# A hybrid decoder trunk: the mixer's parts in another order

## The chip, the cores and the metric

The kernel runs on one core of a Trainium2 chip. The metric is the device time of one execution in microseconds. In the profile PE is TensorE, PEld its weight loads, DVE VectorE, ACT ScalarE, POOL GpSimd, and SP the engine whose queue issues most DMAs; L152 is line 152 of the kernel's file.

## The reference

The trunk has two layers on a sequence of 512 tokens of width 1024. Cut to what matters here, one layer is:

```python
x = x + 0.5 * swiglu(rms_norm(x, ffn1_norm), ffn1_w_in, ffn1_w_out)
z = rms_norm(x, mix_norm) @ mix_w_in          # 1024 -> 772 (FoX) + 768 (MoBA) + 1824 (RWKV)
y = concat([fox_mixer(z_fox), rwkv7_mixer(z_rwkv), moba_mixer(z_moba)]) @ mix_w_out
x = x + y
x = x + memory_cross_attention(rms_norm(x), rms_norm(mem), ...)
x = x + 0.5 * swiglu(rms_norm(x, ffn2_norm), ffn2_w_in, ffn2_w_out)
```

- `fox_mixer`: causal attention of 4 heads of 64 with normalised q and k, and a bias of cumulated log-sigmoid gates (4 columns of z).
- `rwkv7_mixer`: 8 heads of 64. Each projected column is mixed with its value one token earlier. From r, k, v, a decay (a tanh of 64 columns, through w2), a rate a (64 columns, through a2) and a gate g (160 columns, through g2) a state of 64 x 64 per head is carried over the tokens: `state = state * w + (state @ -kk) (kk*a)^T + v k^T`, and `y = state @ r`; then a group norm, a bonus term and the gate.
- `moba_mixer`: attention of 4 heads with rotary positions; at 512 tokens the selected blocks and the own block together are plain causal attention.
- `memory_cross_attention`: 4 heads of 128 over 256 memory tokens.

## The kernel before

Activations lie transposed, features on partitions, 512 tokens along the free axis. A product of full precision is made of three matmuls (`three`, L152 to L154) of a high and a low half of weights and activations. `weights` loads a weight block of 512 KB by SP's queue into `wraw` (three buffers), ACT copies the high half `whi` (L145) and DVE subtracts it for the low half `wlo` (L146), two buffers each.

**Projections of the mixer.** A narrow projection (`zproj`) makes 128 columns for all 512 tokens: 8 pieces of the contraction, 24 matmuls of 512 columns into one PSUM bank. RWKV has 15 of them: R, K and V for each of four pairs of heads (R0 to V3, `rwkv_z`), and three in `rwkv_prep`: the first for decay and rate (`tw`), the second for most of the gate (`gs0`), the third for the rest of the gate and FoX's four gate columns, whose cumulated sums `fox_gates` makes. FoX's q and k are four more (fq0, fq1, fk0, fk1, `heads_t`). A wide projection (`ztok`, L948 to L950) makes 256 columns with the tokens on partitions, 96 matmuls of 256 columns: fv, mv (`values`), mq and mk (`heads`).

**RWKV by pairs.** Each pair of heads passes through six stages, written as generators: `s` (`rwkv_scaled`: norm of k at L641, decay and rate at L650, scaled operands), `g` (`rwkv_gram`, L717: products of the operands, written to DRAM (`scA`), read back as blocks of 16 (`A`), inverted on POOL in 30 small operations (L282) and sent back through DRAM to `Tf` and `Pf`), `r` (`rwkv_rows`), `i` (`rwkv_inverse`, from L809), `t` (`rwkv_transitions`) and `y` (`rwkv_states`: eight steps of the state in a row at L900 and L902, the group norm with DVE's scaling at L920, transposes at L924, and the gate at L930 and L931). `fNM` is one unit of FoX attention: query block N, pair of heads M, with scores (L1034), softmax, transposes (L1022) and the product with the values (L1046).

**The order.** `ORDER` lists the parts of the mixer. `order` gives the n-th part a priority of 1000 n less a lead from `PRI` by its kind; a planner that estimates the time of each instruction then lays the instructions of each engine in order, by priority among those that it takes to be ready. On the chip each engine goes through its list in that order. `ORDER2` does the same for the stage behind (`31` and the like are MoBA units, `m` one step of the memory's keys and values `mem_kv`, `c` a split of outputs, `w` an output projection, `x` the return of x), and `ORDER3` for the cross-attention.

**Memory.** The mixer's eight PSUM banks are `acc` (1), `sp` (2), `tx` (1), `ty` (2) and `ts` (2). Projections use `acc`, but K0 goes to `sp` and the second of `rwkv_prep` to `tx` (`ACC`). `tx` serves stage s, `ty` stages g, r and i, `ts` stages t and y; attention in this stage puts scores, transposes and outputs into `sp`. The next stage has `acc`, `po`, `sp` and `pt`, two banks each. `RPW` and `BPW` say in which of three pools a bank lies, and pools of the same number follow each other in the same memory: a bank of the next stage waits for the one that lay there. `LATE` does the same for SBUF tiles: those of pool 0 lie where the next stage's memory keys and values come, those of pool 2 farther behind. `p` and `pT`, the tiles of every attention unit and of q and k heads, have one buffer each in this stage.

Of the kernel before, what the change touches and what calls it, by code (L numbers as in the profile page):

```python
# [25 lines left out]
PRI = {"s": 1500, "g": 6000, "r": 6000, "i": 10000, "t": -3000, "y": 6000, "p": 4000, "R": 1500, "q": -1500, "f": -1500, "V": 6000, "g1": 2500}  # L26
# [7 lines left out]

ORDER = ("R0 V0 K0 p R1 K1 s0 fk1 g0 V1 r0 fq1 i0 K2 t0 fk0 R2 V2 fq0 s1 g1 r1 i1 fv y0 t1 K3 s2 R3 g2 "
         "f01 r2 mk y1 f11 f00 i2 mq V3 t2 s3 g3 r3 f20 f10 i3 y2 t3 f30 f21 y3 f31 mv")


ORDER2 = "31 11 10 m c0 01 21 00 c1 c2 m c4 x c5 c3 m c6 w3 m 20 m w6 m 30 w4 c7 w1 w5 w2 w0"

ORDER3 = "sum spread z1 z0 n1 z2 n0 m n2 02 z3 00 n3 12 03 10 13 01 11"
BP = {"acc": 2, "po": 2, "sp": 2, "pt": 2}

TAGS = {"s": "tx", "g": "ty", "r": "ty", "i": "ty", "t": "ts", "y": "ts"}

LATE = {"y2": 1, "G": 0, "Pf": 1, "KX": 1, "tk1": 0, "V2": 0, "gs0": 2, "gs1": 2, "ER": 1, "BN": 1, "KV": 2, "AR": 2, "tk2": 1, "g2": 1, "var": 2, "DC": 2, "p": 2, "a": 2, "zr": 0, "e": 0, "lw": 1, "zv": 1, "zk": 0}
RPW = {"ts": 0, "sp": 1, "acc": 0, "tx": 1, "ty": 1}
BPW = {"acc": 0, "sp": 2, "pt": 0, "po": 1}  # L50

RW = {"e": 2, "tk1": 2, "tk2": 2, "zr": 2, "zv": 2, "ER": 2, "zk": 2, "BN": 2}
RP = {"acc": 1, "tx": 1, "ty": 2, "ts": 2, "sp": 2}
# [2 lines left out]
ACC = {"K0": "sp", "p1": "tx"}  # L56
# [59 lines left out]
class Trunk:  # L116
# [405 lines left out]
        nc.vector.scalar_tensor_tensor(out, z[:m, 1:], self.dpar[:m, l, 14 + i:15 + i], out, op0=ALU.mult, op1=ALU.add)  # L522

    def rwkv_prep(self, l, ap, rp, at, ab):
        nc, rw = self.nc, self.rw
        w = self.ins['mix_w_in'][l]
        self.tw = rw.tile([P, S], F32, name="tw", tag="tw")
        self.acc = ACC.get("p0", "acc")
        ps = self.zproj(ap, *self.weights(w[:, Z_LO:Z_LO + P]), P)
        self.shift(l, 12, ps, P, self.tw)  # L530
        nc.scalar.activation(self.tw[0:64], self.tw[0:64], AF.Tanh)
        self.gs = []
        for i, m in ((0, P), (1, 32)):
            g = rw.tile([P, S], F32, name=f"gs{i}", tag=f"gs{i}")
            self.acc = ACC.get(f"p{i + 1}", "acc")
            if i == 0:
                ps = self.zproj(ap, *self.weights(w[:, Z_LO + P:Z_LO + 256]), P)
            else:
                ps = self.zproj(ap, *self.weights(w[:, Z_LO + 256:Z_LO + 288], w[:, 768:772]), 36)
                self.fox_gates(l, ps, rp, at, ab)  # L540
            self.shift(l, 13 + i, ps, m, g[:m])
            nc.scalar.activation(g[:m], g[:m], AF.Tanh, scale=0.5)
            nc.vector.tensor_scalar(g[:m], g[:m], 0.5, 0.5, op0=ALU.mult, op1=ALU.add)
            self.gs.append(g)

    def fox_gates(self, l, ps, rp, at, ab):

# [594 lines left out]
    def mixer_and_xattn(self, l):  # L1142
        tc, nc = self.tc, self.nc

        def sb(name, bufs=1):
            return tc.tile_pool(name=name, bufs=bufs, reuse_waits="tile")

        def pp(name, bufs=1):
            return tc.tile_pool(name=name, bufs=bufs, space=PSUM, reuse_waits="tile")
# [4 lines left out]
        fv = xt[:, 4:6, :].rearrange("p a (b c) -> p (a b) c", c=256)  # L1154
        cqk = xt[:, 6:8, :].rearrange("p a b -> p (a b)").bitcast(BF16).rearrange("p (i a s) -> p i a s", i=2, a=2)
        self.cq, self.ck = cqk[:, 0], cqk[:, 1]
        with sb("raw") as raw:
            mq = raw.tile([P, 2, S], F32, name="mq", tag="mq")
            mk = raw.tile([P, 2, S], F32, name="mk", tag="mk")
            mv = raw.tile([P, NT, 256], F32, name="mvv", tag="mvv")  # L1160
# [6 lines left out]
            with sb("rw") as rw0, sb("rwm") as rw1, sb("rwl") as rw2, pp("rp") as rp0, pp("rps") as rp1, pp("rpt") as rp2:  # L1167
                rp = self.tp = TagPool((rp0, rp1, rp2), RP, where=RPW)
                self.rw = at = TagPool((rw0, rw1, rw2), RW, where=LATE)
                w = self.ins['mix_w_in'][l]  # L1170
                sts = [{} for _ in range(4)]


                steps, begun = [self.norm_sum, self.norm_spread], []

                def z(nm, hp):
                    g = self.rwkv_z(l, hp, rp, "RKV".index(nm))
                    next(g)
                    if steps:
                        steps.pop(0)(self.bank(TAGS["s"], 1)[:, 0])  # L1180
                        begun.append((g, nm, hp))
                        if steps:
                            return
                    for g, nm, hp in begun or [(g, nm, hp)]:
                        sts[hp][nm] = next(g)
                    begun.clear()

                def go(*parts):

                    gens = [f(l, hp, sts[hp]) for f, hp in parts]  # L1190
                    while gens:
                        gens = [g for g in gens if next(g, gens) is not gens]

                early = [0, 0]

                def attend(o):

                    fox, t, pr = o[0] == "f", int(o[1]), int(o[2])
                    q, k, v = (fq, fk, fv) if fox else (mq, mk, mv)
                    if not fox:  # L1200
                        early[pr] += 1
                        assert early[pr] == t + 1
                    self.causal(at, rp, q, k, v, t, pr,
                                lambda ps: self.cp("fo", q[:, pr, t * P:(t + 1) * P], ps), fox)

                def unit_t(*a):
                    self.heads_t(*a)()

                def unit(*a):
                    self.heads(*a)()  # L1210
                scaled, gram, rows = self.rwkv_scaled, self.rwkv_gram, self.rwkv_rows
                inverse, trans, states = self.rwkv_inverse, self.rwkv_transitions, self.rwkv_states
                parts = {"fv": lambda: self.values(l, 0, rp, fv),
                         "mq": lambda: unit(w, 772, 0, rp, at, rp, mq, 64, self.rope(l, 0)),
                         "mk": lambda: unit(w, 772, 1, rp, at, rp, mk, 64, self.rope(l, 1)),
                         "mv": lambda: self.values(l, 772, rp, mv),
                         "p": lambda: self.rwkv_prep(l, rp, rp, at, rp)}
                stages = {"s": scaled, "g": gram, "r": rows, "i": inverse, "t": trans, "y": states}
                for a in range(2):
                    parts[f"fq{a}"] = lambda a=a: unit_t(w[:, a * P:(a + 1) * P], rp, at, rp, fq[:, a], 64, self.dpar[:, l, 12:13])  # L1220
                    parts[f"fk{a}"] = lambda a=a: unit_t(w[:, 256 + a * P:384 + a * P], rp, at, rp, fk[:, a], 64,
                                                         self.par('fox_k_gain', l))
                for o in self.order(ORDER, PRI, lambda o: "q" if o in parts and o != "p" else o[0]):
                    self.acc = ACC.get(o, "acc")
                    if o in parts:
                        parts[o]()
                    elif o[0] in "KRV":
                        z(o[0], int(o[1]))
                    elif o[0] in "fb":
                        attend(o)  # L1230
                    else:
                        go(*[(stages[a[0]], int(a[1])) for a in o.split("+")])
            self.acc = "acc"
            with sb("kv") as kv, pp("bp") as bp0, pp("bps") as bp1, pp("bpt") as bp2:
                bp = TagPool((bp0, bp1, bp2), BP, {"st": "po"}, BPW)
                mem = self.mem_kv(l, kv, bp)
                bank = lambda m: bp.tile([P, 512], F32, name="sp", tag="sp")

                with sb("at") as at_, sb("yy") as yy:
# [4 lines left out]
                    at = TagPool(at_, {**AT, "mx": 2, "sm": 2, "hr": 2})  # L1244
# [5 lines left out]
                    done = set()  # L1250
                    for o in self.order(ORDER2, PRI2, lambda o: "a" if o[0] in "0123" else o[0]):
                        if o == "m":
# [5 lines left out]
                        elif o[0] == "w":  # L1258
                            m = int(o[1])
# [97 lines left out]
```

## Time and profile before

| | us |
|---|---|
| median of 3 runs | 2590.47 |
| lowest and highest | 2580.43, 2592.95 |
| the profiled execution: its time | 2590.88 |
| the profiled execution: span from first to last instruction | 2589.1 |
| PE busy | 2497.2 (96% of the span) |
| DVE, ACT, POOL busy | 1346.6, 846.9, 493.0 |

The span is what the trace covers, and the time of the execution is a little longer. Matmuls are pipelined, so a busy PE is not a PE at its peak; the granted clock tells how fast it was allowed to run.

### The profile page before, as it was taken

What the parts mean: (1) busy time and instruction counts of PE and PEld (TensorE: products, weight loads), DVE (VectorE), ACT (ScalarE), POOL (GpSimd) and SP (SyncE); (2) the same over time, 40 slices, a digit from 0 to 9 for tenths busy, and PEclk for the clock granted to TensorE, in tenths of its full rate; (3) what the DMA queues carried; (4) which work ended last, traced back from release to release, by engine and by line L of the source; (5) the groups of instructions that cost most, each with busy time, mean ns of one, the idle gap of its engine ahead of it and who ended that gap; (6) DMA issues with size and microseconds to landing.
All of it is one profiled execution on the core that took longest, in us unless ns stands there. A gap on an engine that the chain in (4) does not pass through costs nothing.

```text
span 2589.1 us, 35163 instructions
## 1 busy us (share of the span) xinstructions
PE 2497.2 (96%) x13976; PEld 2025.7 (78%) x13976; DVE 1346.6 (52%) x2503; ACT 846.9 (33%) x1337; POOL 493.0 (19%) x610
## 2 busy tenths in 40 slices
PE   8999998899999899999999999999999899999999
PEld 7888876787667788888888888767877677888887
DVE  6444445666755654344444444465666666543444
ACT  4222233233343342222332222333333433422222
POOL 4212120232210122020221211202322110221211
PEclk9999999998889999999999999999978999999999
DMA  4333342221213133333333333422212121333332
GB/s 143 104 98 94 96 130 69 66 59 43 64 34 92 53 96 90 104 93 98 95 94 100 94 98 94 121 75 58 67 34 56 56 78 45 110 98 98 95 95 88
DMA packets 434880, 218.41 MB, mean 84 GB/s; under 512 B 63856, under 2 KB 428828, under 8 KB 434716
## 3 DMA queue, kind: packets, MB, share of 16 engines
q1 hardware_dynamic: 431948, 212.36, 28.9%
q10 hardware_dynamic: 2448, 2.76, 0.3%
q8 instruction: 110, 1.80, 0.3%
q0 software_dynamic: 320, 1.05, 0.1%
q14 instruction: 54, 0.44, 0.1%
HBM read 205.64 MB, written 10.49 MB: 83 GB/s over the span
## 4 chain that ended last, share of the span: by engine, by line
PE 86%; DVE 6%; POOL 3%; DMA 2%; ACT 2%; issue 1%; SPq 1%; POOLq 0%; ACTq 0%; DVEq 0%
PE acc L152 22%; PE acc L154 22%; PE acc L153 22%; PE po L1046 2%; PE sp L1034 1%; POOL P L282 1%; PE pt L1022 1%; PE acc L950 1%; PE acc L948 1%; PE acc L949 1%; POOL T L282 1%; DVE wlo L146 1%; ACT whi L145 1%; PE ts L857 1%; PE ty L717 1%
## 5 line engine op out<-in xcount | busy, mean ns | idle before, releaser
L145 ACT ACTIVATE whi<-wraw 128x1024 fp32r<-128x1024 f32 (+3 forms) x386 | 390.3, 1013 | 1142.0 <-PE acc L153 1043.3
L152 PE MATMUL acc<-xh,whi 128*128 128x512 f32 (+1 forms) x1776 | 699.9, 394 | 21.9 <-DVE p L496 7.3
L154 PE MATMUL acc<-xh,wlo 128*128 128x512 f32 (+1 forms) x1776 | 695.8, 392 | 1.3 <-DVE wlo L146 1.3
L153 PE MATMUL acc<-xl,whi 128*128 128x512 f32 (+1 forms) x1776 | 694.8, 391 | 0.0
L146 DVE TENSOR_TENSOR wlo<-wraw,whi 128x1024 fp32r<-128x1024 f32 (+3 forms) x386 | 540.3, 1401 | 100.3 <-ACT whi L145 91.4
L152 PEld LDWEIGHTS acc<-xh,whi 128*128 128x128 f32 (+1 forms) x1776 | 334.4, 188 | 97.6 <-ACT whi L145 9.1
L154 PEld LDWEIGHTS acc<-xh,wlo 128*128 128x128 f32 (+1 forms) x1776 | 334.2, 188 | 75.5 <-DVE wlo L146 2.6
L153 PEld LDWEIGHTS acc<-xl,whi 128*128 128x128 f32 (+1 forms) x1776 | 334.6, 188 | 69.7
L342 POOL TENSOR_TENSOR up<-up,g 128x512 f32<-128x512 f32 x88 | 118.4, 1346 | 999.2 <-ACT whi L145 901.1
L152 PE MATMUL acc<-th,whi 128*128 128x512 f32 x704 | 274.4, 391 | 1.0 <-ACT whi L145 1.0
L154 PE MATMUL acc<-th,wlo 128*128 128x512 f32 x704 | 275.0, 392 | 0.2
L153 PE MATMUL acc<-tl,whi 128*128 128x512 f32 x704 | 274.0, 389 | 0.0
L295 DVE SCALAR_TENSOR_TENSOR x<-acc,x 128x512 f32<-128x512 f32 x96 | 66.0, 691 | 277.2 <-PE acc L154 277.2
L341 DVE TENSOR_TENSOR up<-acc,rsb 128x512 f32<-128x512 f32 x88 | 60.8, 691 | 278.5 <-PE acc L154 278.5
L338 DVE TENSOR_TENSOR g<-acc,rsb 128x512 f32<-128x512 f32 x88 | 60.8, 691 | 191.0 <-PE acc L154 188.0
L154 PEld LDWEIGHTS acc<-th,wlo 128*128 128x128 f32 x704 | 132.1, 188 | 31.5 <-DVE wlo L146 4.2
L152 PEld LDWEIGHTS acc<-th,whi 128*128 128x128 f32 x704 | 132.2, 188 | 30.5 <-ACT whi L145 4.0
L153 PEld LDWEIGHTS acc<-tl,whi 128*128 128x128 f32 x704 | 132.2, 188 | 27.4
L240 POOL TENSOR_TENSOR sqacc<-sqacc,sq 128x512 f32<-128x512 f32 x48 | 75.4, 1571 | 381.6 <-ACT sq L239 245.9
L346 POOL TENSOR_TENSOR tl<-up,th 128x512 fp32r<-128x512 f32 x88 | 128.5, 1461 | 65.5 <-ACT th L345 65.5
L345 ACT ACTIVATE th<-up 128x512 fp32r<-128x512 f32 x88 | 55.8, 634 | 120.8 <-POOL up L342 120.8
L948 PE MATMUL acc<-whi,xh 128*128 128x256 f32 x256 | 76.9, 300 | 0.7 <-DVE zt L520 0.7
(351 smaller groups left out, 3109.1 us busy)
## 6 DMA issues: line engine op xcount, KB each, us to landing
wraw<-in_ffn_w_in_dram SPq DMA_DIRECT2D x176, 512.0 KB
wraw<-in_ffn_w_out_dram SPq DMA_DIRECT2D x64, 512.0 KB
wraw<-in_mix_w_in_dram SPq DMA_DIRECT2D x52, 512.0 KB
wraw<-in_ffn_w_out_dram SPq DMA_DIRECT2D x32, 384.0 KB
wraw<-in_xattn_w_kv_dram SPq DMA_DIRECT2D x16, 512.0 KB
wraw<-in_mix_w_out_dram SPq DMA_DIRECT2D x16, 384.0 KB
scx<-x SPq DMA_DIRECT2D x16, 256.0 KB
x<-scx SPq DMA_DIRECT2D x16, 256.0 KB
```

The lines of the kernel that those rows point to most:

```text
L145: nc.scalar.activation(hv, v, AF.Copy)
L146: nc.vector.tensor_sub(lv, v, f32(hv))
L152: mm(ps, lh, rh, start=start, stop=False)
L153: mm(ps, lh, rl, start=False, stop=False)
L154: mm(ps, ll, rh, start=False, stop=stop)
L240: (nc.vector if m == KC - 1 else nc.gpsimd).tensor_tensor(self.sqacc, self.sqacc, sq, op=ALU.add)
L295: self.nc.vector.scalar_tensor_tensor(xm, ps, coef, xm, op0=ALU.mult, op1=ALU.add)
L338: nc.vector.tensor_tensor(g, pss[0], rsb, op=ALU.mult)
L341: nc.vector.tensor_tensor(up, pss[1], rsb, op=ALU.mult)
L342: nc.gpsimd.tensor_tensor(up, up, g, op=ALU.mult)
L346: nc.gpsimd.tensor_tensor(tl, up, f32(th), op=ALU.subtract)
L948: mm(o, a, wh[:, kk, :], start=k == 0, stop=False)
```

## The change

`ORDER` and `ORDER2` are other lists. `rwkv_prep` becomes a generator of three steps, so that its projections are three parts of the list (p0, p1, p2) in place of one (p); each keeps its bank. K0 and R0 stand first, p0 and V0 next, and then stage s of pair 0. FoX's, MoBA's and the gate's projections stand farther behind. Four of the small placements change with it.

```diff
-ORDER = ("R0 V0 K0 p R1 K1 s0 fk1 g0 V1 r0 fq1 i0 K2 t0 fk0 R2 V2 fq0 s1 g1 r1 i1 fv y0 t1 K3 s2 R3 g2 "
-         "f01 r2 mk y1 f11 f00 i2 mq V3 t2 s3 g3 r3 f20 f10 i3 y2 t3 f30 f21 y3 f31 mv")
+ORDER = ("K0 R0 p0 V0 s0 K1 R1 g0 p1 r0 V1 i0 p2 t0 s1 K2 g1 R2 y0 r1 V2 i1 fk1 s2 t1 fq1 K3 g2 R3 y1 r2 V3 i2 fv "
+         "s3 t2 f01 fk0 g3 fq0 y2 r3 f11 f00 mk i3 f10 f21 mq mv t3 f20 f31 y3 f30")
-ORDER2 = "31 11 10 m c0 01 21 00 c1 c2 m c4 x c5 c3 m c6 w3 m 20 m w6 m 30 w4 c7 w1 w5 w2 w0"
+ORDER2 = "m 31 11 m 10 c0 01 m 21 c1 c2 00 c4 x m c5 c3 w3 20 c6 m w6 30 m w4 c7 w1 w5 w2 w0"
-LATE = {... "p": 2, "a": 2, ...}
-RPW = {"ts": 0, "sp": 1, "acc": 0, "tx": 1, "ty": 1}
-BPW = {"acc": 0, "sp": 2, "pt": 0, "po": 1}
+LATE = {... "p": 2, "pT": 2, "a": 2, ...}
+RPW = {"acc": 0, "tx": 0, "ty": 0, "sp": 1, "ts": 2}
+BPW = {"acc": 0, "pt": 0, "sp": 1, "po": 2}
...
     def rwkv_prep(self, l, ap, rp, at, ab):
-        self.acc = ACC.get("p0", "acc")
         ps = self.zproj(ap, *self.weights(w[:, Z_LO:Z_LO + P]), P)
         self.shift(l, 12, ps, P, self.tw)
         nc.scalar.activation(self.tw[0:64], self.tw[0:64], AF.Tanh)
+        yield
         self.gs = []
         for i, m in ((0, P), (1, 32)):
-            self.acc = ACC.get(f"p{i + 1}", "acc")
...
             self.gs.append(g)
+            yield
...
+                prep = self.rwkv_prep(l, rp, rp, at, rp)
-                         "p": lambda: self.rwkv_prep(l, rp, rp, at, rp)}
+                         **{f"p{i}": lambda: next(prep) for i in range(3)}}
-                for o in self.order(ORDER, PRI, lambda o: "q" if o in parts and o != "p" else o[0]):
+                for o in self.order(ORDER, PRI, lambda o: "q" if o in parts and o[0] != "p" else o[0]):
```

## Rows read from the trace of the kernel before

**Rows 1.** The page: span, and granted clock in 40 slices (tenths).
```profile
span 2589.1 us, 35163 instructions
...
PEclk9999999998889999999999999999978999999999
```

**Rows 2.** Stretches: length, busy (count) of PE PEld DVE ACT POOL, PEclk, DMA.
```profile
387.00:600.00 213.00, 197.33 (x1456) 158.79 (x1456) 129.34 (x320) 67.30 (x106) 42.56 (x95) 0.96 0.26 64
600.00:686.00 86.00, 83.07 (x830) 69.00 (x828) 62.24 (x162) 28.57 (x64) 19.55 (x45) 0.94 0.15 34
686.00:757.50 71.50, 60.71 (x500) 38.47 (x499) 39.36 (x117) 28.69 (x66) 15.64 (x33) 0.78 0.15 43
757.50:870.00 112.50, 108.01 (x594) 84.85 (x593) 68.37 (x165) 46.02 (x92) 13.09 (x9) 0.99 0.30 92
...
1666.80:1880.00 213.20, 196.53 (x1453) 158.14 (x1454) 129.25 (x320) 67.32 (x106) 42.66 (x95) 0.96 0.26 64
1880.00:1966.00 86.00, 81.60 (x779) 68.32 (x779) 57.73 (x150) 26.81 (x60) 18.32 (x46) 0.86 0.15 35
1966.00:2039.00 73.00, 63.82 (x555) 45.05 (x555) 41.25 (x128) 30.40 (x69) 15.19 (x30) 0.84 0.17 41
```

**Rows 3.** The stretch from 600, instructions of L152, then of L948: PE, PEld.
```profile
600.00:757.50 157.50, 3.33 (x8) 1.50 (x8) 0.87 0.15 38
...
600.00:757.50 157.50, 16.09 (x54) 10.45 (x54) 0.87 0.15 38
```

**Rows 4.** Timeline of POOL: start, us, engine line op out<-in shapes xcount [idle before <-releaser].
```profile
475.84 0.22 POOL L282 TENSOR_TENSOR T<-A,P 64x15 f32<-64x15 f32 x1 [6.65 <-DMA A<-scA]
...
480.68 1.35 POOL L282 TENSOR_TENSOR P<-P,T 64x63 f32<-64x63 f32 x1
...
617.98 0.41 POOL L282 TENSOR_TENSOR P<-P,T 64x63 f32<-64x63 f32 x1
```

**Rows 5.** Timeline of PE, pair 0: last gram matmuls and first of the inverse.
```profile
465.17 1.79 PE L717 MATMUL ty<-ER,B 64*128 64x128 f32 x16 [1.00 <-DVE BN L721]
...
496.64 0.33 PE L809 MATMUL ty<-Tf,tk 64*64 64x64 f32 x2 [2.52 <-DMA Tf<-scT]
```

**Rows 6.** Timeline of PE, end of layer 0's mixer.
```profile
727.33 1.12 PE L1034 MATMUL sp<-fox 64*128 64x512 f32 x2
...
731.87 0.60 PE L1022 MATMUL pt<-ident,p 128*128 128x128 f32 x4
...
736.33 1.09 PE L1046 MATMUL po<-pT,fox 128*64 128x128 f32 x8
...
751.07 1.09 PE L924 MATMUL ts<-ident,tk 128*128 128x128 f32 x4 [4.14 <-DVE tk L920]
...
755.79 1.97 PE L1022 MATMUL pt<-ident,p 128*128 128x128 f32 x8
757.55 1.91 PE L1075 MATMUL acc<-ident,mtk 128*128 128x128 f32 x8
```

**Rows 7.** Timeline of DVE: a weight split, and a MoBA unit's last scaling.
```profile
480.62 1.23 DVE L146 TENSOR_TENSOR wlo<-wraw,whi 128x1024 fp32r<-128x1024 f32 x1 [0.22 <-ACT whi L145]
...
745.59 0.35 DVE L1019 TENSOR_SCALAR p<-p,sm 128x256 f32<-128x256 f32 x1
```

**Rows 8.** Timeline of PE: V0's first matmul, and the first of pair 0.
```profile
396.54 0.50 PE L152 MATMUL acc<-xh,whi 128*128 128x512 f32 x1 [2.35 <-DVE zt L520]
...
441.74 0.95 PE L641 MATMUL tx<-blk,e 128*128 128x2 f32 x8
```

**Rows 9.** Timeline of PE: a projection's first matmul, and what follows its last.
```profile
447.82 0.50 PE L152 MATMUL acc<-xh,whi 128*128 128x512 f32 x1 [0.43 <-DVE p L496]
...
453.43 0.95 PE L502 MATMUL sp<-blk,p 128*128 128x2 f32 x8
```

**Rows 10.** Two stretches around a fall of the clock, columns as in rows 2.
```profile
580.00:589.20 9.20, 9.20 (x104) 8.19 (x103) 6.57 (x11) 4.43 (x7) 2.92 (x2) 1.00 0.17 47
589.20:599.40 10.20, 10.20 (x51) 8.18 (x50) 4.75 (x12) 1.32 (x2) 1.30 (x2) 0.50 0.21 63
```

More of the change, by code (lines that the diff above doesn't have):

```diff
@@ L46 @@
 TAGS = {"s": "tx", "g": "ty", "r": "ty", "i": "ty", "t": "ts", "y": "ts"}
-LATE = {"y2": 1, "G": 0, "Pf": 1, "KX": 1, "tk1": 0, "V2": 0, "gs0": 2, "gs1": 2, "ER": 1, "BN": 1, "KV": 2, "AR": 2, "tk2": 1, "g2": 1, "var": 2, "DC": 2, "p": 2, "a": 2, "zr": 0, "e": 0, "lw": 1, "zv": 1, "zk": 0}
-RPW = {"ts": 0, "sp": 1, "acc": 0, "tx": 1, "ty": 1}
-BPW = {"acc": 0, "sp": 2, "pt": 0, "po": 1}
+LATE = {"y2": 1, "G": 0, "Pf": 1, "KX": 1, "tk1": 0, "V2": 0, "gs0": 2, "gs1": 2, "ER": 1, "BN": 1, "KV": 2, "AR": 2, "tk2": 1, "g2": 1, "var": 2, "DC": 2, "p": 2, "pT": 2, "a": 2, "zr": 0, "e": 0, "lw": 1, "zv": 1, "zk": 0}
+RPW = {"acc": 0, "tx": 0, "ty": 0, "sp": 1, "ts": 2}
+BPW = {"acc": 0, "pt": 0, "sp": 1, "po": 2}
 RW = {"e": 2, "tk1": 2, "tk2": 2, "zr": 2, "zv": 2, "ER": 2, "zk": 2, "BN": 2}
```

## The prediction

> **What bounds the kernel now.** I read the page first: the span is 2589.1 us, and TensorE's granted clock dips only in two places [rows 1]. They are the two layers' mixers, so I cut one into stretches and looked at two losses in each: the time in which PE is not busy, and the share of the clock not granted [rows 2]. The two levels are 1.2 and 2.4 GHz, so a granted 0.78 is full clock for 56% of a stretch and half clock for 44%; where PE is busy, one minus the granted clock, times the length, is the time that half clock costs. In layer 0:
>
> - 387 to 600: idle 213.0 - 197.3 = 15.7, clock 0.04 x 213 = 8.5, together 24.2 us or 11.4%.
> - 600 to 686: 2.9 + 5.2 = 8.1 us, 9.4%.
> - 686 to 757.5: 10.8 + 15.7 = 26.5 us, 37%.
>
> Layer 1 gives 25.2 (11.8%), 16.4 (19%) and 20.9 us (29%). A mixer thus loses 58.8 and 62.5 us, 121 together. The end is set by PE's work plus such losses, and the worst stretch is the last of each mixer.
>
> Why the last: a mixer has 19 narrow projections (24 matmuls, 8 of them on line 152) and 4 wide ones (96 matmuls, 32 on line 948). Behind 600 us lie 8 of 152 and 54 of 128 [rows 3], one narrow and 1.7 wide. What is left for the end is the chain of RWKV's pair 3, with attention. One pair's chain is long and mostly not PE's: in pair 0 the last gram matmuls begin at 465.17, the blocks are back from DRAM at 475.84, POOL inverts, and the inverse begins at 496.64 [rows 4, 5]: 30 us. At the very end PE waits 4.14 us for DVE's scaling behind the group norm [rows 6]. The next stage can't fill that wait: a MoBA unit's probabilities are ready at 745.94, yet the transposes of the MoBA units start at 755.79, right behind the last `ts` work, and the memory's at 757.55 [rows 6, 7]. Their banks lie where `ts` and `acc` were, and pair 3 holds `ts` to the end.
>
> **The change part by part.**
>
> *Instructions.* The yields and the new lists add and remove none: the same 23 projections, weight loads on SP's queue and gates, and the same banks for K0 and p1. All is order, memory placement, and what these let overlap.
>
> *Pair 0 begins earlier.* Before, its first own matmul comes at 441.74 [rows 8], behind R0, V0, K0, p0, p1, p2, R1 and K1. Now `s0` needs K0, R0, p0 and V0 only. A narrow projection takes 5.6 us (447.82 to 453.43) [rows 9], four fewer some 22 us, so I expect it at about 420. The chains of pairs 0 and 1 can then be covered by K1, R1, V1, p1, p2, K2, R2 and V2, 45 us against a chain's 30. On SP's queue a pair's block transfers now stand among more weight loads, and a load waits for the split of older weights; behind it the blocks wait, then POOL, then PE. The bound above is the 2.52 us wait for `Tf` [rows 5] once more in each of three pairs, 7.6 us a layer and 15 in all; below, nothing. I take nothing, since pair 0 already has loads around it and its wait is in the loss of the first part, which I use below.
>
> *The start.* Before, R0 and V0 share one `acc` bank, and V0 waits 2.35 us for R0's eviction, which waits for the broadcast norm [rows 8]. Now K0 (bank `sp`) goes first, R0 follows at once, and the norm can be there at its end; p0 still waits for R0's eviction, as the 0.43 us at 447.82 [rows 9]. Gain 1.9 us a layer, 3.8 in all; bounds 0 and 4.7.
>
> *Projections moved back.* fk0, fq0, mk, mq and mv now stand behind pair 3's gram. A wide matmul has half the columns of a narrow one, so I estimate 96 x 5.6/24/2 = 11.2 us for a wide projection. Three wide and two narrow are 45 us of dense matmuls in the last part, where before 5.6 + 1.7 x 11.2 = 25 us stood. Pair 3's own R, K and V come earlier, so its chain can run beside them.
>
> *The hand-over.* `acc`, `tx` and `ty` now lie under the next stage's `acc` and `pt`, and `ts` under its `po`; `pT` moves to the late memory. So the memory's projections, now first in the next list, need not wait for pair 3's last matmul nor the last `pT`. They are work moved, not saved: the stretch that they leave loses only 4.5 + 1.1 of 112.5 us [rows 2] and keeps the output projections. If it runs short of cover there, the loss reappears there; the bound is the 4.14 us wait of before.
>
> *POOL.* An inversion is 30 small operations in a row. One of them took 1.35 us in pair 0 while DVE split weights (480.62 to 481.85) and 0.41 in pair 2, away from projections [rows 4, 7]. Three splits beside an inversion are some 3 us more. I take nothing, hidden by PE's work as long as that lasts; uncovered in one pair of each layer it is +6. The Trainium skill (SBUF — State Buffer, section "SBUF: two separate sides") gives the cause: a VectorE operation with two SBUF inputs and a GpSimd operation that reads SBUF shut each other out for a whole instruction. By that rule each projection's weight split holds up the inversion beside it, which speaks against this change, and the trace agrees at 480.68; the sum by it would be the 6 us higher.
>
> *The sum.* PE's work at full clock is 370.5 - 58.8 = 311.7 us in layer 0 and 372.2 - 62.5 = 309.7 in layer 1. Dense matmuls beside pairs' chains is what the first part has today, and it loses 11.4 to 11.8%. I take 11.6% for the whole new mixer: 311.7/0.884 = 352.6 (-17.9) and 309.7/0.884 = 350.3 (-21.9). With the start, -43.6 us. The profiled execution took 2590.88 us (its span and 1.8), against a median of 2590.47; 2590.9 - 43.6 = 2547, and I say 2548. Bounds of the share: the 5% of the stretch behind the mixer gives -89, today's 16% nothing.
>
> **The rivals.**
>
> *The half clock only moves (2584).* Idle time is not all that matters to the clock: from 580.0 to 589.2 PE was busy 9.20 of 9.20 us, with 104 mostly small matmuls, and ran the next 10.2 us at half clock [rows 10]. With two pairs' small matmuls side by side and fewer projections among them, half clock may go to the first part. Then only idle time is saved: 27.3 us in the later parts, which at the first part's 7.4 to 7.8% would be 24, so -3, and the start: 2584. Against it: R, K, V and p still lie in the first part.
>
> *The clock follows idle time alone (2525).* Then filling PE's long waits gives all half clock back: (8.5 + 5.2 + 15.7) + (8.5 + 12.0 + 11.7) = 61.6 us, and the start: 2525. Against it stands the fall at 589.2, with no wait before it. The Trainium skill (TensorE: Matmul & The Clock Gate, section "Why this matters for your kernels") advises against idle gaps between bursts of matmuls; the row at 589.2 shows a fall without one, so this gets little.
>
> *Attention piles up at the end (2615, slower).* In this stage `p` and `pT` have one buffer each, and attention, fk, fq, mk and mq all pass through them. A FoX unit of four blocks runs from 727.33 to 737.42, 10.1 us, in which PE has 2 x 1.12 + 2 x 0.60 + 2 x 1.09 = 5.6 us of its own [rows 6]. FoX needs fk1, fq1, fv and p2, which now come later. If its units fall behind, the last ones stand alone: each then costs 4.5 us idle and, at half clock, 5.6 more. The last stretches lose 26.5 + 20.9 = 47.4 us now. It decides from 47.4/2/10.1 = 2.3 units alone behind a layer's last dense projection: three make 61, +13 or 2604; four make 81, +33 or 2624. For it: the list ends t3, f20, f31, y3, f30. Against: memory projections and MoBA units can now run beside them.
>
> **How the numbers follow.** The forecast's case (2530 to 2570) 0.55; half clock moves (2570 to 2600) 0.18; clock follows idle time (below 2530) 0.13; pile-up (above 2600) 0.14. A measurement tells this kernel from no change at about 0.5%, 13 us: below 2577.5 or above 2603.4. Faster are the first and third and a little of the second, 0.69; within 0.5% most of the second and the edge of the last, 0.18; slower 0.13. The range takes in the bounds of SP, POOL and the start around the forecast and the next cases, cutting the outer part of the two far ones: 2520 to 2600.
>
> **What would show it.** Right: pair 0's first square-sum matmul near 420; no 2.35 us wait behind the norm; memory transposes before the last `ts` matmul; some 352 us from the first projection to the end of pair 3; clock losses of a layer well below 29 us. Wrong: clock losses as large but earlier; a wait for `Tf` in every pair; FoX units alone at the end.

## The result: slower, and the profile after

The changed kernel takes 2664.93 us (median of 4, 2657.91 to 2670.61), against 2591.71 us for the kernel before beside it. The ratio is 1.0288, 95% interval 1.0244 to 1.0331. The profiled execution took 2661.48 us.

The page of the changed kernel, as [rows 1]:

```profile
span 2659.7 us, 35149 instructions
...
PEclk9999999889999999999999999988989799999999
```

The dips of the clock have not gone: in the first mixer two slices stand below 9 where there were three, in the second four where there were two. Stretches of the changed kernel, columns as in [rows 2]:

```profile
387.00:600.00 213.00, 189.54 (x1360) 144.84 (x1359) 124.42 (x297) 63.47 (x102) 39.72 (x100) 0.88 0.22 53
600.00:686.00 86.00, 83.25 (x801) 69.17 (x801) 50.44 (x152) 28.19 (x59) 23.51 (x65) 0.94 0.22 47
686.00:742.00 56.00, 51.81 (x521) 44.52 (x516) 36.65 (x96) 18.76 (x42) 6.61 (x5) 0.97 0.13 39
742.00:776.00 34.00, 26.72 (x123) 16.43 (x120) 19.82 (x48) 15.72 (x36) 7.82 (x5) 0.85 0.25 72
776.00:897.00 121.00, 113.15 (x594) 86.88 (x594) 70.23 (x170) 44.88 (x91) 9.59 (x6) 0.97 0.26 83
1693.00:1906.00 213.00, 189.66 (x1332) 144.78 (x1331) 123.45 (x293) 62.87 (x101) 38.38 (x94) 0.86 0.22 54
1906.00:1992.00 86.00, 82.71 (x717) 69.27 (x716) 45.86 (x140) 23.22 (x52) 24.77 (x70) 0.86 0.22 46
1992.00:2060.00 68.00, 62.53 (x626) 53.17 (x625) 42.91 (x114) 24.42 (x52) 6.30 (x5) 0.97 0.11 33
2060.00:2096.00 36.00, 29.51 (x119) 18.39 (x118) 19.66 (x48) 15.55 (x35) 7.74 (x5) 0.69 0.23 71
2096.00:2224.00 128.00, 120.33 (x597) 90.62 (x596) 70.88 (x171) 45.16 (x91) 9.55 (x6) 0.93 0.25 77
```

Loss is reckoned as in the prediction: idle time, plus length times one minus the granted clock. Layer 0, with [rows 2] for before:

| stretch | before | after | difference |
|---|---|---|---|
| first part (387 to 600) | 24.2 | 23.5 + 25.6 = 49.0 | +24.8 |
| rest of the mixer (to 757.5; to 742) | 34.6 | 6.9 + 6.8 = 13.8 | -20.8 |
| FoX units alone (742 to 776) | - | 7.3 + 5.1 = 12.4 | +12.4 |
| next stage | 5.6 | 7.9 + 3.6 = 11.5 | +5.9 |

Layer 1 gives +28.0 in the first part, -14.5 in the rest, +17.7 and +11.5, where its next stage before lost 5.2 (2037.5 to 2148.0). Together the loss grew by some 65 of the 70.6 us by which the two profiled spans differ; 41 of these are half clock, 24 idle time. The part that the prediction set out to mend gave back 35 us; the first part, on whose share it had built its sum, took 53.

The stretches are cut by time, and not all hold the same work before and after. From 387 to the end of pair 3 the changed kernel does 355 - 62.8 = 292 us of PE's work at full clock in layer 0, where before it did 311.7; the rest has moved behind pair 3.

Three places in the trace of the changed kernel. TensorE's timeline, columns as in [rows 4]:

```profile
397.40 0.45 PE L257 MATMUL tx<-ident,rs 128*128 128x128 f32 x1 [4.09 <-DVE rs L270]
402.39 0.77 PE L153 MATMUL acc<-xh,whi 128*128 128x512 f32 x1 [3.89 <-DVE zt L521]
410.72 0.39 PE L643 MATMUL tx<-blk,e 128*128 128x2 f32 x3
...
476.24 0.33 PE L811 MATMUL ty<-Tf,tk 64*64 64x64 f32 x2 [1.51 <-DMA Tf<-scT]
...
739.03 1.12 PE L933 MATMUL ts<-gs,g 32*128 32x512 f32 x2
...
743.27 0.91 PE L1036 MATMUL sp<-fox 64*128 64x384 f32 x2 [0.50 <-ACT mq L276]
...
767.32 3.26 PE L1048 MATMUL po<-pT,fox 128*64 128x128 f32 x16
...
773.62 1.12 PE L1036 MATMUL sp<-mk,mq 64*128 64x512 f32 x2
```

*Start.* K0 and R0 stand back to back, but the sum of squares comes behind both, and PE waits 4.09 and 3.89 us where it had waited 2.35 [rows 8]. Still pair 0's first matmul is at 410.72 in place of 441.74. *Middle.* VectorE's timeline, and then, of the changed kernel, the stretch from 526.5 to 553 with the instructions of L153, the first matmul of every narrow projection's group of three:

```profile
514.13 0.68 DVE L497 TENSOR_TENSOR p<-acc,rsb 128x512 f32<-128x512 f32 x1
...
552.70 0.69 DVE L497 TENSOR_TENSOR p<-acc,rsb 128x512 f32<-128x512 f32 x1
```

```profile
526.50:553.00 26.50, 0.05 (x1) 0.00 (x0) 0.72 0.17 38
```

fk1 takes the only tile `p` at 514.13; fq1 gets it at 552.70, and until then its result stands in the only `acc` bank. No projection runs, and the clock is 0.72. *End.* The last `ts` matmuls end at 740.2, 16 us earlier than before, but three FoX units follow, to 770.6, with only a few transposes of the memory beside them, and the first MoBA scores come at 773.62. The load of the memory's rows, a row on ACT's queue, is issued only now too, as mv's last matmuls end; before, it was issued at 685.21, there too at the end of mv:

```profile
741.81 0.40 ACTq L1067 DMA_DIRECT2D mtk<-in_mem_dram  x1
```

### The profile page after: what moved, and what is told of

Read it like the earlier page. It is cut to its first block, busy times and chain, and to the rows that moved or that the text cites. A ratio compares the mean times of both kernels' runs of the same rounds, so it can differ in the third digit from the quotient of the medians.

```text
span 2659.7 us, 35149 instructions
## 1 busy us (share of the span) xinstructions
PE 2544.9 (96%) x13976; PEld 2055.1 (77%) x13976; DVE 1355.4 (51%) x2503; ACT 845.9 (32%) x1337; POOL 486.4 (18%) x610
## 4 chain that ended last, share of the span: by engine, by line
PE 88%; DVE 5%; ACT 2%; DMA 2%; issue 2%; POOL 1%; SPq 1%; ACTq 0%; DVEq 0%; POOLq 0%
PE acc L153 23%; PE acc L155 22%; PE acc L154 22%; PE po L1048 2%; PE sp L1036 1%; PE acc L950 1%; PE acc L951 1%; PE acc L952 1%; PE ty L719 1%; DVE wlo L147 1%; PE pt L1024 1%; ACT whi L146 1%; PE ts L859 1%; PE sp L153 1%; PE ts L902 1%
## 5 line engine op out<-in xcount | busy, mean ns | idle before, releaser
L146 ACT ACTIVATE whi<-wraw 128x1024 fp32r<-128x1024 f32 (+2 forms) x386 | 390.0, 1012 | 1144.6 <-PE acc L154 1060.7
L153 PE MATMUL acc<-xh,whi 128*128 128x512 f32 (+1 forms) x1776 | 706.0, 398 | 22.5 <-DVE zt L521 11.7
L147 DVE TENSOR_TENSOR wlo<-wraw,whi 128x1024 fp32r<-128x1024 f32 (+2 forms) x386 | 545.1, 1413 | 105.7 <-ACT whi L146 96.1
L153 PEld LDWEIGHTS acc<-xh,whi 128*128 128x128 f32 (+1 forms) x1776 | 337.9, 190 | 105.4 <-ACT e L640 8.5
L153 PE MATMUL acc<-th,whi 128*128 128x512 f32 x704 | 274.4, 391 | 1.0 <-ACT whi L146 1.0
L153 PEld LDWEIGHTS acc<-th,whi 128*128 128x128 f32 x704 | 132.2, 188 | 30.7 <-ACT whi L146 4.0
L950 PE MATMUL acc<-whi,xh 128*128 128x256 f32 x256 | 77.9, 304 | 7.2 <-ACT p L969 5.3
```

Of the source, the lines that this page charges most:

```text
L146: nc.scalar.activation(hv, v, AF.Copy)
L147: nc.vector.tensor_sub(lv, v, f32(hv))
L153: mm(ps, lh, rh, start=start, stop=False)
L950: mm(o, a, wh[:, kk, :], start=k == 0, stop=False)
```

## The experiments

All ratios are against the kernel before, timed beside the run, with the 95% interval. In the diffs only the part of a list that differs is shown.

### Which part of the change costs

`a_oldord`: everything as changed, but the mixer's list of before.

```diff
-ORDER = ("K0 R0 p0 V0 s0 K1 R1 g0 p1 ...
+ORDER = ("R0 V0 K0 p0 p1 p2 R1 K1 s0 fk1 g0 ...   (as before)
```

> The changed kernel (its memory placement, its list for the next stage, its three steps of p) with the mixer's list of before, p0 p1 p2 standing where p stood. If the mixer's list alone is what costs: 2585 to 2595 us, as before, or below it by what the earlier banks give. If the placement or the next stage's list cost too, part of the 73 us stays: 2600 us or more. A theory of the whole change as one (half clock from the pairs running ahead) expects the former.

Measured: 1.0102 (1.0076 to 1.0128). `b_place` and `b_ord2` split that:

```diff
 b_place: the kernel before with
+LATE = {... "p": 2, "pT": 2, ...}
+RPW = {"acc": 0, "tx": 0, "ty": 0, "sp": 1, "ts": 2}
+BPW = {"acc": 0, "pt": 0, "sp": 1, "po": 2}
 b_ord2: the kernel before with
+ORDER2 = "m 31 11 m 10 c0 01 m 21 c1 c2 00 c4 x m c5 c3 w3 20 c6 m w6 30 m w4 c7 w1 w5 w2 w0"
```

> The kernel before with the changed placement alone (LATE, RPW, BPW). Theory 'MoBA's score banks': with the lists of before the changed placement and next list cost 1.0% together; before, the MoBA units' score banks lay where tx and ty had been and three units' scores ran from 738 us, under the tail of pair 3; now they lie in FoX's own score banks, and the first MoBA scores come at 749.5 and one unit after the other. Then the placement alone costs 8 us a layer, ratio 1.005 to 1.01. Rival 'next list': the memory first, MoBA later is what costs, and placement alone gives 0.997 to 1.003.

> The kernel before with the next stage's list of the change alone (ORDER2). Theory 'MoBA's score banks': the list alone costs little, 0.998 to 1.004, since the banks let the units begin as before. Rival 'next list': 1.006 to 1.01.

Measured: b_place 1.0046 (1.0026 to 1.0066), b_ord2 1.011 (1.0055 to 1.0165). So with the list of before both cost, and they do not add up: both together are a_oldord's 1.0102. b_ord2 speaks for the rival "next list" and against "MoBA's score banks"; b_place lies between the two. The first MoBA scores of the kernel before, then of a_oldord, b_place and b_ord2:

```profile
738.16 0.70 PE L1034 MATMUL sp<-mk,mq 64*128 64x512 f32 x2
```

```profile
749.50 1.12 PE L1036 MATMUL sp<-mk,mq 64*128 64x512 f32 x2
```

```profile
747.46 1.13 PE L1035 MATMUL sp<-mk,mq 64*128 64x512 f32 x4
```

```profile
749.25 2.07 PE L1034 MATMUL sp<-mk,mq 64*128 64x512 f32 x2
```

Before, these scores ran under pair 3's tail. The placement alone and the next list alone each put them off by 9 to 11 us, so the delay is not the banks' doing alone. `a_oldback` has the new mixer list alone (and the split p), on the placement and next list of before:

```diff
 a_oldback: the changed kernel with LATE, RPW, BPW and ORDER2 of before
```

> The changed mixer list alone, on the placement and the next list of before. The other two alone measured 1.005 and 1.011, both with the list of before 1.010. If the three parts add up: 1.0288 / 1.010, a ratio of 1.016 to 1.021. Theory 'the parts belong together' (the new list ends with FoX units whose score banks and ts the new placement keeps apart from the next stage): 1.025 or more without them.

Measured: 1.0295 (1.0246 to 1.0344). The mixer's list alone is enough for the whole damage. The three parts do not add up: with this list, whose end is FoX's units, the placement and the next list change nothing more that the intervals show, while with the list of before they cost 1%.

### Single stops undone

`a_start`:

```diff
-ORDER = ("K0 R0 p0 V0 s0 ...
+ORDER = ("R0 K0 p0 V0 s0 ...
```

> The changed kernel with R0 ahead of K0 again; all else as changed. Theory 'three local stops': with K0 first, its priority number stands behind that of R0's matmuls, so the sum of squares is issued behind both projections and the two waits of 4.09 and 3.89 us follow; the first 25 us of a mixer lose 11.5 us where before they lost 4.1. Putting R0 first gives back about 7 us a layer: 14 us, some 2651 us, and the waits at the first spread and at the next projection shrink below 2.5 us together. Rival 'half clock in general': two pairs' small matmuls side by side are what the clock falls on, and the start is a few us at most: 2660 to 2665 us.

Measured: 1.0259 (1.0233 to 1.0286). This lies between the two theories. The stretch from 385 to 410 in a_start, then in the changed kernel and in the kernel before:

```profile
385.00:410.00 25.00, 22.60 (x102) 18.62 (x101) 12.28 (x33) 7.16 (x9) 0.29 (x3) 0.93 0.33 92
```

```profile
385.00:410.00 25.00, 17.02 (x67) 13.80 (x66) 6.90 (x18) 4.77 (x6) 0.20 (x2) 0.73 0.24 66
```

```profile
385.00:410.00 25.00, 20.86 (x95) 16.52 (x95) 10.41 (x22) 6.45 (x9) 0.30 (x3) 1.00 0.29 68
```

The order of K0 and R0 is the cause there: 14.7 us lost become 4.2, about the 4.1 of before. Of the 21 us that this would be in two layers the whole kernel gives back 0.3%, about a third, and the intervals overlap, so even that is not shown.

`a_ptag` lets fq0 and fq1 work in the tile that attention uses later:

```diff
+self.ptag = "pT" if o in ("fq0", "fq1") else "p"
-t = at.tile([P, 2, S], F32, name="p", tag="p")
+t = at.tile([P, 2, S], F32, name="p", tag=getattr(self, "ptag", "p"))
```

> The changed kernel with fq0 and fq1 working in the tile pT (idle until attention begins) and not in p; all else as changed. Theory 'three local stops': from 519 to 553 us no projection runs, because fq1's result stands in the only acc bank until fk1 lets go of the only p tile (552.70). With another tile the bank is free some 30 us earlier, dense matmuls stand in this stretch, its half clock goes (538 to 558 us), and 410 to 600 us loses up to 12 us less, in layer 1 up to 16 less: 2637 to 2650 us. Rival 'half clock in general': the projections that move forward are missing further back, the half clock moves there, and the time stays within 5 us of 2665.

Measured: 1.0288 (1.0252 to 1.0323), no gain. Three stretches of layer 0 of a_ptag, then the same of the changed kernel, columns as in [rows 2]:

```profile
505.00:545.00 40.00, 38.89 (x289) 30.61 (x288) 25.50 (x53) 12.60 (x22) 10.28 (x26) 1.00 0.19 50
...
625.00:665.00 40.00, 36.16 (x298) 27.11 (x294) 25.84 (x72) 7.34 (x21) 8.33 (x21) 0.70 0.06 12
...
745.00:785.00 40.00, 33.30 (x139) 21.98 (x139) 18.49 (x48) 14.60 (x33) 3.75 (x4) 0.66 0.16 53
```

```profile
505.00:545.00 40.00, 34.84 (x292) 27.00 (x290) 29.13 (x75) 14.91 (x28) 9.22 (x20) 0.91 0.20 52
...
625.00:665.00 40.00, 38.90 (x425) 31.75 (x424) 26.91 (x87) 9.41 (x21) 7.85 (x20) 0.87 0.11 27
...
745.00:785.00 40.00, 33.22 (x177) 22.76 (x176) 23.77 (x60) 17.23 (x42) 4.87 (x3) 0.87 0.28 89
```

The blocked stretch is healed, from 0.91 to 1.00 and 4 us more busy; in this layer loss turns up at 625 (0.87 to 0.70) and at 745 (0.87 to 0.66). Layer 1, from the mixer's start to the end of the next stage, in a_ptag and then in the changed kernel:

```profile
1697.90:2204.10 506.20, 465.07 (x3389) 362.72 (x3388) 301.29 (x764) 169.98 (x328) 90.87 (x182) 0.92 0.23 60
```

```profile
1688.30:2218.30 530.00, 486.10 (x3387) 377.48 (x3387) 303.06 (x764) 169.76 (x327) 87.21 (x182) 0.88 0.22 57
```

Here the loss did not come back: 107.5 us became 81.6. So the rows of layer 0 alone do not show that the loss always moves; that undoing this stop gains nothing is shown by the timed ratio.

`a_tail` and `a_mvearly` change the end of the list, `a_fix` joins a_start and a_ptag:

```diff
-a_tail:    ... f10 f21 mq mv t3 f20 f31 y3 f30
+a_tail:    ... f10 f21 f20 mq f31 t3 f30 y3 mv
-a_mvearly: ... i2 fv s3 t2 ... mq mv t3 ...
+a_mvearly: ... i2 fv mv s3 t2 ... mq t3 ...
```

> The changed kernel with the FoX units of the end drawn forward and mq and mv put between and behind them (f21 f20 mq f31 t3 f30 y3 mv). Theory 'three local stops': three FoX units stand alone behind mv for 34 us and lose 11.9 us, in layer 1 15.9; with mv last, dense matmuls fill their waits: 10 to 25 us less, 2640 to 2655 us. Rival 'the memory part waits for mv': mtk is loaded into room that mv's inputs hold, so a later mv puts the memory's transposes and projections off by as much, and the next stage loses what the mixer gains: 2660 to 2675 us.

> The changed kernel with mv drawn forward behind fv, so that the last reader of xl is done earlier and the memory's rows can be loaded before pair 3 ends. Theory 'late attention': the memory's projections can then stand beside the three FoX units at the end, 8 to 12 us a layer: ratio 1.019 to 1.023. Theory 'cover is only moved': what mv covered from 722 to 742 us is bare then: 1.025 to 1.033.

> The changed kernel with two stops undone together: R0 ahead of K0, and fq0 and fq1 in the tile pT. Theory 'bare chains lose' (each stop's gain turns up as a loss elsewhere): 1.023 to 1.029. Rival 'single stops add up': the 7 us a layer of the start and the 12 to 16 of the blocked bank, 1.010 to 1.018.

Measured: a_tail 1.0309 (1.0275 to 1.0343), a_mvearly 1.0374 (1.0333 to 1.0414), a_fix 1.0247 (1.0214 to 1.0279). a_tail gained nothing, as its rival had it. a_mvearly lies outside both its expectations: mq became the last reader of xl, and the memory's load came at 733.6, only 8 us earlier, so that run says little on the memory's wait. a_fix lies where "bare chains lose" put it. The theory of three local stops falls: two of them undone together give 0.4%, with overlapping intervals, where 1.1 to 1.9% was expected if single stops add up.

### The early pair and the late projections, each alone

`b_early` draws pair 0 forward in the kernel before; `a_late` undoes that in the changed kernel and leaves FoX's projections late.

```diff
 b_early, on the kernel before
-R0 V0 K0 p R1 K1 s0 fk1 g0 V1 r0 fq1 i0 K2 t0 ...
+R0 V0 K0 p0 s0 p1 R1 g0 K1 p2 r0 fk1 V1 i0 fq1 K2 t0 ...
 a_late, on the changed kernel
-K0 R0 p0 V0 s0 K1 R1 g0 p1 r0 V1 i0 p2 t0 s1 ...
+R0 V0 K0 p0 p1 p2 R1 K1 s0 g0 r0 V1 i0 t0 s1 ...
```

> The kernel before (its placement and next list) with pair 0 alone drawn forward: R0 V0 K0 p0 s0 p1 R1 g0 K1 p2 r0 fk1 V1 i0 fq1 K2 t0, then as before. The prediction's step (pair 0's chain about 20 us earlier, covered by projections) expects 5 to 20 us less: ratio 0.992 to 0.998. Theory 'cover is only moved' (the dense work is the same in sum; what is drawn to one place is missing at another): the end is not set by pair 0's start, 0.998 to 1.005.

> The changed kernel with the first part's start undone: R0 V0 K0 p0 p1 p2 R1 K1 stand ahead of s0 as before, V0's and the norm's order too; all behind as changed (FoX's, MoBA's projections late, the three FoX units at the end, the changed placement). Theory 'what is late costs, not what is early': ratio 1.015 to 1.028, the start's 7 us a layer given back and no more. Rival 'the early pairs cost': most of the change goes, 1.000 to 1.012.

Measured: b_early 1.0195 (1.0163 to 1.0228), a_late 1.0441 (1.0406 to 1.0477), both outside every expectation. Each half alone is slower than before, and the late half alone is worse than the whole change. One row of b_early's PE timeline, and pair 3's stretch in b_early and then before:

```profile
428.35 1.01 PE L717 MATMUL ty<-ER,B 64*128 64x128 f32 x6 [6.87 <-DVE B L281]
```

```profile
705.00:778.20 73.20, 64.76 (x497) 43.65 (x498) 36.19 (x114) 25.72 (x60) 9.69 (x24) 0.72 0.08 17
```

```profile
705.00:755.90 50.90, 45.37 (x417) 28.81 (x416) 26.56 (x86) 19.91 (x47) 2.86 (x3) 0.80 0.04 9
```

Only p1 stands on PE between pair 0's first matmuls and its gram, whose lead in PRI is 6000, six places of the list; R1 follows behind. So PE waits 6.87 us for DVE with projections behind the waiting matmul in its queue. Pair 0's first matmul comes 33 us earlier, and pair 3's last 22 us later (778.2 against 755.9). The changed kernel has no such wait: there four projections stand between pair 0's first matmul (410.72) and its gram (440.48), so b_early is slow in part for a reason of its own. In a_late the stretch from 505 to 545, all instructions, and those of L152:

```profile
505.00:545.00 40.00, 31.47 (x316) 26.40 (x316) 11.27 (x27) 6.47 (x15) 3.35 (x12) 0.54 0.22 40
```

```profile
505.00:545.00 40.00, 0.00 (x0) 0.00 (x0) 0.54 0.22 40
```

Pair 0's and pair 1's chains stand there without a projection, and 8.5 + 18.4 = 26.9 of 40 us are lost. Before, fk1, fq1, fk0, fq0 and fv covered these chains.

### FoX's units

`a_nofox` and `b_nofox` leave the eight FoX units of a layer, and so their output, out of either list:

```diff
 a_nofox, b_nofox: ORDER without f01 f11 f00 f10 f21 f20 f31 f30
```

> The changed kernel with the eight FoX units of a layer left out (their output is missing; all projections and gates stay). To be read against the same cut in the kernel before. Theory 'late attention': FoX begins at 583 us in place of 530 and its last three units stand behind the last projection; without the units the two kernels differ by less than 25 us in place of 73. Theory 'cover is only moved': pairs 0 and 1 miss the FoX projections that covered them, whether the units are there or not; the difference stays above 45 us.

> The kernel before with the eight FoX units of a layer left out, the counterpart of the run above. Its units stand beside pairs 2 and 3 in a stretch where PE is busy; both theories expect 25 to 60 us less than before.

Measured: a_nofox 1.007 (1.0036 to 1.0104), b_nofox 0.9911 (0.9877 to 0.9945). The two differ by 2597.80 - 2559.94 = 38 us in place of 73, between the two expectations. Some 23 of the 38 us stand in the next stage, where the changed placement and next list are at work too. This stage in a_nofox, then in b_nofox, layer 0:

```profile
758.80:875.90 117.10, 110.97 (x534) 81.76 (x535) 67.81 (x167) 41.52 (x87) 14.95 (x11) 0.92 0.25 77
```

```profile
745.60:856.20 110.60, 108.54 (x586) 84.59 (x585) 68.75 (x163) 43.84 (x90) 14.80 (x11) 0.98 0.29 90
```

It loses 15.5 against 4.3 us here, and 16.1 against 4.3 in layer 1. In the kernel before sixteen units cost 0.9% (23 us, a little below the 25 to 60 expected), in the changed one 1.0288 - 1.007 = 2.2% (56 us). A stretch of b_nofox, with no projection in it, shows why they are so cheap before:

```profile
665.00:745.60 80.60, 66.93 (x535) 51.61 (x531) 31.69 (x107) 23.35 (x53) 13.74 (x36) 0.58 0.08 15
```

The end of pair 2 and pair 3, without the units, lose 13.7 + 33.9 = 47.5 of 80.6 us, 59%; with the units beside them, again without a projection, the last stretch of before loses 37% [rows 2]. So I drew the units forward in the changed list:

```diff
 a_foxfwd on the changed kernel, b_foxfwd with the placement and next list of before
+R0 K0 p0 V0 s0 K1 R1 g0 p1 r0 V1 i0 p2 t0 fk1 s1 K2 g1 fq1 R2 y0 r1 fv V2 i1 f01 s2 t1 fk0 K3 f11 g2 R3 y1
+fq0 r2 f21 V3 i2 f00 mk s3 t2 f10 g3 mq f31 y2 r3 f20 i3 t3 f30 y3 mv
```

> The changed kernel (its placement and next list, pair 0 early, R0 ahead of K0) with FoX's projections and units drawn forward, so that all eight units stand beside pairs 1 to 3 and none behind y3; mk, mq and mv stay late. Theory 'FoX's units need the pairs' waits beside them': the 35 us that the units cost more than before go, and 7 of the start: ratio 1.005 to 1.015. Rival 'dense cover alone counts' (FoX's projections, moved forward, are missing at the end): 1.020 or more.

> The same list on the placement and the next list of before. Theory 'FoX's units need the pairs' waits beside them': as the run above, and up to 10 us a layer less, since with FoX done early the next stage can begin as it did before: 0.995 to 1.010. Rival 'dense cover alone counts': 1.020 or more.

Measured: a_foxfwd 1.0415 (1.0375 to 1.0456), b_foxfwd 1.0297 (1.026 to 1.0334). The theory of the late units falls too. b_foxfwd, first a row of PE's timeline, then stretches; last the next stage of a_foxfwd:

```profile
466.84 0.47 PE L809 MATMUL ty<-Tf,tk 64*64 64x64 f32 x2 [7.42 <-DMA Tf<-scT]
```

```profile
425.00:505.00 80.00, 67.96 (x507) 50.61 (x509) 39.79 (x110) 18.27 (x30) 17.53 (x44) 0.81 0.19 47
...
625.00:781.40 156.40, 135.88 (x1200) 103.47 (x1200) 88.81 (x261) 52.79 (x117) 25.91 (x43) 0.85 0.13 35
781.40:892.20 110.80, 108.28 (x585) 84.55 (x586) 68.92 (x163) 43.79 (x90) 14.76 (x11) 0.98 0.29 90
```

```profile
785.30:904.20 118.90, 111.11 (x534) 83.34 (x534) 68.27 (x167) 41.64 (x87) 15.76 (x11) 0.90 0.25 75
```

In b_foxfwd the next stage is as before (2.5 + 2.2 us lost). In a_foxfwd, with the same list on the changed placement and next list, it loses 7.8 + 11.9. So these two cost that stage 15 us without any FoX unit behind pair 3; twice that is about the 1.2% between the two runs. FoX at the end is a second cause: in a_oldback, on the placement and next list of before, 31 us are lost between pair 3's end and the end of that stage (748.0 to 904.2), where before lost 4. In b_foxfwd pair 0's chain is bare (7.42 us for its blocks, 27 of 80 us lost), and pair 3 ends at 781, again later than before.

### Cover by itself

`a_fill` and `b_fill` add three dummy narrow projections a layer, `b_spread` moves three projections of the kernel before back:

```diff
+if o[0] == "d":
+    self.zproj(rp, *self.weights(w[:, Z_LO:Z_LO + P]), P, (self.xh, self.xh))
 a_fill:   ... t3 f20 d0 f31 d1 y3 f30 d2
 b_fill:   ... y2 t3 d0 f30 d1 f21 d2 y3 f31 mv
-b_spread: ... t0 fk0 R2 V2 fq0 s1 ... s2 R3 g2 f01 r2 mk y1 f11 f00 i2 mq V3 t2 s3 g3 r3 ...
+b_spread: ... t0 R2 V2 s1 ... s2 fk0 R3 g2 f01 r2 fq0 mk y1 f11 f00 i2 V3 t2 s3 g3 mq r3 ...
```

> The changed kernel with three dummy narrow projections a layer (24 dense matmuls each, weights loaded and split like others, nothing reads the result) among the three FoX units at the end: 3 x 5.6 = 16.8 us of dense work a layer at full clock, 33.6 in all, or 1.3% of the time. Theory 'bare chains lose': the stretch from 742 to 776 us lost 11.9 us in layer 0 and 15.9 in layer 1, so the dummies cost less than half of their own time: ratio 1.029 to 1.035. Rival 'PE's time is what counts, wherever it stands': the full price, 1.040 to 1.044.

> The kernel before with three dummy narrow projections a layer listed among pair 3's last stages, 33.6 us of dense work in all. They come ahead of mv, so that dense work reaches further into the last part, which lost 37% and 29%. Theory 'bare chains lose': less than half of their time, 1.000 to 1.006. Rival 'PE's time is what counts': 1.011 to 1.015.

> The kernel before with four FoX and MoBA projections drawn apart: fk0 behind s2, fq0 behind r2, mq behind g3; pairs 1 and 2 move up in the list for it. In 505 to 585 us before, 47 of 80 us are dense and nothing is lost to the clock; from 585 on dense work is thin. Theory 'bare chains lose': if enough cover is left in front, 5 to 15 us less, 0.994 to 0.998; if the front goes bare, 1.000 to 1.010. It beats both kernels only in the first case.

Measured: a_fill 1.0364 (1.0328 to 1.0399), b_fill 1.0088 (1.0061 to 1.0114), b_spread 1.0193 (1.0155 to 1.0232). The dummies cost 22.7 of their 33.6 us in b_fill and 0.76% or 19.6 in a_fill, between the two theories' bounds, so neither is borne out as it was put. In b_fill the interval leaves out the full price, 1.3%; in a_fill the two intervals do not. The two mixers of b_fill, then of before:

```profile
383.00:764.10 381.10, 358.22 (x2868) 283.37 (x2867) 231.91 (x602) 126.98 (x238) 72.86 (x170) 0.93 0.23 57
...
1670.00:2056.60 386.60, 356.83 (x2877) 281.62 (x2876) 233.62 (x605) 129.34 (x241) 72.58 (x172) 0.95 0.23 57
```

```profile
383.00:755.90 372.90, 343.42 (x2797) 267.97 (x2796) 230.83 (x598) 124.98 (x235) 76.15 (x170) 0.92 0.22 54
...
1661.00:2037.30 376.30, 345.92 (x2805) 274.58 (x2804) 229.85 (x601) 126.35 (x238) 74.92 (x173) 0.92 0.22 55
```

The loss of the two mixers falls from 59.3 + 60.5 to 49.6 + 49.1 us: added dense work does pay back. By the timed ratio it pays back 10.9 of its 33.6 us, about a third. b_spread, meant to beat both kernels, lost 1.9%, outside both its expectations. No run that does all of the work came below the kernel before.

## Why the prediction was wrong

- **Pair 0 begins about 420:** right in kind, 410.72. That it helps is not borne out: in b_early the early pair, with its own wait at the gram, costs 1.95%, and pair 3 ends later, not earlier. There pair 3's end is not set by where pair 0 begins.
- **Some 352 us from the first projection to the end of pair 3:** it came out in layer 0 (387 to 742 is 355 us, and 367 in layer 1), and that is luck. The prediction had 311.7 us of work at 11.6% lost; the runs have 292 us at 17.7%, and the missing work follows behind pair 3.
- **The cover, 45 us of projections against a chain of 30:** wrong in the changed kernel on one count: one `acc` bank and one `p` keep listed projections from running (none from 526.5 to 553). b_early shows another, that a place in the list is not a place on PE (the leads put the gram ahead of R1); in the changed kernel pair 0's gram had its projections ahead of it.
- **The transfers on SP's queue, and POOL, at nothing:** right. PE waits for `Tf` 2.0 us in layer 0 and 2.3 in layer 1 (the longest of layer 0 is the 1.51 shown), less than the 4.1 and 5.3 before. The Trainium skill's rule (SBUF — State Buffer, "SBUF: two separate sides"), by which each weight split holds up an inversion, made no wait of PE here that I could find; no run tested it by itself.
- **The start, +1.9 us a layer:** wrong in sign. Its first 25 us lose 14.7 us, where before lost 4.1; a_start shows the order of K0 and R0 as the cause there.
- **Projections moved back:** right. The rest of the mixer lost 20.8 and 14.5 us less.
- **The hand-over, "work moved, not saved", bound 4.14 us:** mis-sized. FoX's units alone and the next stage lose 18.3 and 29.2 us more. In this the rival of the pile-up was right, with three units alone, as it named them; but it priced them at 61 us for two layers, where they lost 12.4 + 17.7 = 30, and as the whole of the damage. In a_tail another order of the end gave nothing back.
- **The sum, 11.6% for the whole new mixer: this step failed.** It carries the share of the first part over, "dense matmuls beside pairs' chains is what the first part has today". Measured, the new mixer lost 17.7% (62.8 of 355 us) and 20.7% (76.0 of 367) to the end of pair 3, and 19.3% and 23.2% with the FoX units behind it. Even the first part, where the share came from, lost 23% and 25%: the change takes covering work from it. The first matmuls of the groups of three, before (L152, L948) and then after (L153, L950), from 387 to 600:

```profile
387.00:600.00 213.00, 55.71 (x136) 25.48 (x136) 0.96 0.26 64
...
387.00:600.00 213.00, 22.50 (x74) 15.06 (x74) 0.96 0.26 64
```

```profile
387.00:600.00 213.00, 55.59 (x128) 25.49 (x127) 0.88 0.22 53
...
387.00:600.00 213.00, 4.25 (x15) 2.85 (x15) 0.88 0.22 53
```

17 narrow and 2.3 wide projections became 16 and 0.5: by the prediction's 5.6 and 11.2 us, 121 us of dense work became 95, and the loss went from 24.2 to 49.0. Of the 24.8 us more, 10.6 are the start. A hint of this stood in the prediction's own numbers: 19 narrow and 4 wide are 151 us, or 43% of a mixer of 352.6, where the first part had 121 of 213, 57%. The share of the whole mixer before, 58.8 of 370.5 or 16%, would have forecast no gain. But the share of dense work does not by itself give the loss: from 600 to 742 the changed kernel has 2 narrow and 3.6 wide projections, some 51 of 142 us or 36%, and loses 9.7%. That the missing cover is the cause of the first part's loss is thus argued from these rows and from a_late, and not shown by itself.

The rival "the half clock only moves" named half clock in the first part, and that came. But it did not only move: in the stretches of the table and their counterparts of layer 1 half clock costs 105 us where it cost 64. Shown is this much: the mixer's list alone is enough for the difference; without FoX's units about half of it goes, and some 23 of the 38 us that stay are lost in the next stage; chains without projections or units lose a half and more of their time, and units or dense work beside them reduce that. Open is which arrangement would gain, and how the first part's loss divides between missing projections and the order of the pairs: drawing the units forward gave nothing. A second `p` buffer was not tried.

## What to carry to other kernels

A loss share read in one stretch belongs to that stretch's mix: before carrying it over, count the covering work that the whole has, and what the edit takes from the stretch itself. Where independent dense work is fixed in sum, an order is judged by what stands bare after the move; healing the worst stretch or one visible stop says little, and only the whole time tells. A mark that comes out as forecast (here pair 3's end) says little either, unless the same work lies ahead of it.

## What the runs showed of the hardware

- Equal waits, unequal clock: from 745 to 785 PE is idle 6.8 us in the changed kernel and 6.7 in a_ptag, and the granted clock is 0.87 and 0.66. Idle time alone does not set which of the two levels is granted. The Trainium skill (TensorE: Matmul & The Clock Gate, "Why this matters for your kernels") warns of idle gaps; [rows 10] show that to avoid them is not enough: 9.20 of 9.20 us busy, and half clock right behind.
- The two layers run the same program, and in the changed kernel the stretch of three FoX units has nearly the same idle time (7.3 and 6.5 us) at 0.85 and 0.69. Differences of some 10 us in one layer of one profile are thus no evidence by themselves; what is concluded above goes by the timed ratios.
